# Summing modulation rows over partitions on GpSimd instead of TensorE, in a diffusion trunk layer

## The chip, the cores and the metric

The kernel runs on one core of a Trainium2 chip. The core has TensorE (PE in the profile; PEld is its weight load), VectorE (DVE), ScalarE (ACT), GpSimd (POOL), and SyncE (SP), which here only issues transfers. Each engine works through its own queue in order, and semaphores tie the queues together. The metric is the device time of one execution in microseconds (us), taken as the median of several runs.

## The reference

Two groups of tokens, 128 context tokens and 256 latent tokens, pass through one layer with the same weights. Each group has a conditioning vector, and from it come six modulation rows of 2048 numbers:

```
def modulation(cond, w_mod, b_mod):
    m = jax.nn.silu(cond) @ w_mod + b_mod
    return jnp.split(m[..., None, :], 6, axis=-1)
...
    sh1, sc1, g1, sh2, sc2, g2 = modulation(cond, w_mod_l, b_mod_l)
    h = rms_norm(x, n1) * (1 + sc1) + sh1
    q, k, v, u = project_in(h, w_in_l, qg_l, kg_l)
    attn = attend(q, k, v)
    x = x + g1 * token_mixing(h, attn, u, w_na_proj_l, w_fnet_proj_l, w_gate_l, w_o_l)
    h2 = rms_norm(x, n2) * (1 + sc2) + sh2
    x = x + g2 * swiglu(h2, w_gu_l, w_down_l)
```

Rows 0 and 1 (`sh1`, `sc1`) are needed at once. Rows 2 to 5 (`g1`, `sh2`, `sc2`, `g2`) are needed later, and the change is about these four. A row is a vector times a 2048 x 2048 matrix, for two vectors.

## The kernel before

Nearly all time goes into matmuls of 384 tokens with float32 weights. A product is made in three matmuls (`mm3`, lines 165 to 167): weights and activations are split into a high part (`wh`, `hH`, a rounded copy by ACT, line 161) and a low part (`wl`, `hL`, the rest, subtracted by DVE, line 162), and high times high, high times low and low times high are summed. The weights come in units of 256 x 512 numbers. Before a unit is multiplied, `next_unit` splits the one after it; `wh` and `wl` have three buffers each, so the splitting runs ahead of TensorE by up to two units. A unit is 18 matmuls in most stages.

The stages follow each other: the input projection (with rows 0 and 1 made on TensorE), the gate projection with the Fourier part and the attention woven in, the two branch projections, the output projection with the residual, and the feed-forward part to the end.

The four late rows are made beside these stages. `mod_rows` is a generator: whenever the stage takes a unit, `Paced` advances it by some steps (`RATES`, `CHUNKS`), and each step records a little work in the engines' queues at that place. So the order in each queue is set by where these steps fall. The order of the rows is 2, 4, 3, 5. Each row is made in two parts (`cc`) of 1024 columns, eight parts in all. For a part:

- 16 tiles `wm` of the matrix (128 x 1024, 512 KB each, named `wmr` in the profile) are loaded by SP.
- For each tile and each of the two vectors (`cnd`), DVE multiplies the tile with one number per partition and adds it to the accumulator `acc` (`accr` in the profile, 128 x 2 x 1024), line 347. The first tile only multiplies (line 345).
- TensorE sums the 128 partitions with four matmuls against a tile of ones (line 356); ACT copies the result out of PSUM (line 360), and DVE adds it to `row`, which holds the bias (line 362). `row` was reset by a memset on POOL (line 330) and filled with the bias by four small transfers (line 335).
- POOL issues four transfers of the sums to DRAM, `s_row` (line 367).

Rows 4 and 3 are needed as columns: `columns` loads the row back as 32 x 128 (`colr`, line 373) and TensorE transposes it (line 380) into a PSUM tile, from which DVE writes `msc` or `msh`. Rows 2 and 5 are needed as rows, broadcast to all partitions: `load_rows` has SP load them from `s_row` into `gb` (line 1159), for the output projection and for the end of the feed-forward part. `rows_until` advances the generator until a row is recorded, if a stage needs it before.

Of the kernel before, what the change touches and what calls it, by code (L numbers as in the profile page):

```python
# [6 lines left out]

# [25 lines left out]
CH = 512  # L33
# [15 lines left out]
RATES = [1.5, 0.5, 1.1, 1.07, 0.452]  # L49
# [70 lines left out]
def trunk_kernel(ctx: ExitStack, tc: tile.TileContext, io: dict):  # L120
    nc = tc.nc
# [13 lines left out]
    b_mod = io["b_mod"][0]  # L135
# [20 lines left out]
    def nm(s):  # L156
        return f"{s}{next(ids)}"
# [91 lines left out]
    def new_h(kt):  # L249
# [6 lines left out]
    s_row = {  # L256
        ty: [dram.tile([1, D], F32, tag=f"row{ty}{c}", name=f"s_row{ty}{c}") for c in range(2)] for ty in (2, 3, 4, 5)
    }
# [18 lines left out]
    rows_psum, rows_done = {}, set()  # L277
    rpool = None
# [5 lines left out]
    with ExitStack() as ph:  # L284
# [6 lines left out]
        def at_tile():  # L291
            return pa.tile([P, CH], F32, tag="at", name=nm("at"))
# [8 lines left out]
        def acc_tile():  # L301

            return next(ring)()
# [5 lines left out]
        ROWS = (2, 4, 3, 5)  # L309

        def row_weights():


            def load(ty, cc, k):
                wm = rpool.tile([P, 2, CH], F32, tag="wm", bufs=3, name=nm("wmr"))
                c0 = ty * D + cc * 2 * CH
                nc.sync.dma_start(
                    wm, w_mod[k * P : (k + 1) * P, c0 : c0 + 2 * CH].rearrange("p (i n) -> p i n", i=2)
                )
                return wm  # L320

            return Ahead(load, [(ty, cc, k) for ty in ROWS for cc in range(2) for k in range(KT)], 3)

        def mod_rows(ty, src):


            for cc in range(2):
                acc = rpool.tile([P, 2, 2, CH], F32, tag="acc", name=nm("accr"))
                row = rpool.tile([P, CH], F32, tag="row", name=nm("row"))
                nc.gpsimd.memset(row, 0.0)  # L330
                b = b_mod[ty * D + cc * 2 * CH : ty * D + (cc + 1) * 2 * CH].rearrange("(i n) -> i n", i=2)
                for cnd in range(2):
                    for i in range(2):
                        q = 64 * cnd + 32 * i
                        nc.gpsimd.dma_start(row[q : q + 1], b[i : i + 1])
                for k in range(KT):
                    _, wm = src.take()
                    for cnd in range(2):
                        if cnd:
                            if ty != ROWS[0] or cc + k:  # L340
                                src.more()
                            yield
                        sc = csz[:, k, cnd : cnd + 1]
                        if k == 0:
                            nc.vector.tensor_scalar_mul(acc[:, cnd], wm, sc)
                        else:
                            nc.vector.scalar_tensor_tensor(  # L347
                                out=acc[:, cnd], in0=wm, scalar=sc, in1=acc[:, cnd], op0=ALU.mult, op1=ALU.add
                            )
                    yield  # L350
                yield
                o = rows_psum["tile"]()
                for cnd in range(2):
                    for i in range(2):
                        q = 64 * cnd + 32 * i
                        nc.tensor.matmul(
                            o[q : q + 32], ones, acc[:, cnd, i], start=True, stop=True,
                            tile_position=(0, q), skip_group_check=True,
                        )
                nc.scalar.copy(acc[:, 0, 0], o)  # L360
                yield
                nc.vector.tensor_add(row, row, acc[:, 0, 0])
                for cnd in range(2):
                    for i in range(2):
                        q = 64 * cnd + 32 * i
                        c0 = (2 * cc + i) * CH
                        nc.gpsimd.dma_start(s_row[ty][cnd][:, c0 : c0 + CH], row[q : q + 1])

        def columns(ty):

            r = rpool.tile([32, P], F32, tag="colr", name=nm("colr"))
            for cnd in range(2):
                nc.gpsimd.dma_start(
                    r[16 * cnd : 16 * cnd + 16], s_row[ty][cnd].rearrange("o (k p) -> (o k) p", p=P)
                )
            yield
            yield
            yield
            o = rows_psum["tile"]()
            nc.tensor.transpose(o[:, 0:32], r, ident[:32, :32])  # L380
            ov = o[:, 0:32].rearrange("p (c k) -> p k c", c=2)
            yield
            if ty == 3:
                nc.vector.tensor_copy(msh[1], ov)
                return
            nc.vector.scalar_tensor_tensor(
                out=msc[1], in0=ov, scalar=1.0, in1=ng[:, 1].unsqueeze(2).to_broadcast([P, KT, 2]),
                op0=ALU.add, op1=ALU.mult,
            )
# [5 lines left out]
        def mod_weights(alloc):  # L395


            def load(kt0, n, k0):
                w, nk = n * P, depth_of(n)
                wm = alloc([P, 2, nk, w], "wm")  # L400
                for ty in range(2):
                    col = ty * D + kt0 * P
                    nc.sync.dma_start(
                        wm[:, ty],
                        w_mod[k0 * P : (k0 + nk) * P, col : col + w].rearrange("(k p) n -> p k n", p=P),
                    )
                return wm

            return Ahead(load, [(kt0, n, k0) for kt0, n in MODS for k0 in range(0, KT, depth_of(n))], 0)
# [46 lines left out]
        with ExitStack() as pha:  # L456
# [21 lines left out]
            src = mod_weights(wme)  # L478
# [11 lines left out]
            for j in range(2):  # L490
# [10 lines left out]
                out=csz[:, :, 0:2], in_=pt[:, 0:32].rearrange("p (c k) -> p k c", c=2), func=AF.Silu  # L501
# [5 lines left out]
            for cc in range(4):  # L507
                xT.append(c6([P, 4, TOK], "xT"))
                for k in range(4):
                    o = acc_tile()  # L510
# [3 lines left out]
                for t in (1, 2, 0):  # L514
                    junk = tmp.tile([P, CH], F32, tag="junk", bufs=1, name=nm("junk"))
                    nc.scalar.activation(
                        out=junk, in_=xc[cc][:, t], func=AF.Square, accum_out=ssx[:, t, cc : cc + 1]
# [14 lines left out]
            o = at_tile()  # L532
# [68 lines left out]
            prep = Paced(prepare())  # L601
            rows_psum["tile"] = md_tile

            def rows_and_columns():
                src = row_weights()
                yield
                for ty in ROWS:
                    yield from mod_rows(ty, src)
                    if ty in (3, 4):
                        yield  # L610
                        yield from columns(ty)
                    rows_done.add(ty)
                    yield

            rows = Paced(rows_and_columns(), RATES[0])

            def rows_until(ty):
                while ty not in rows_done:
# [15 lines left out]
            acc = {}  # L634
# [400 lines left out]
        for fc8 in range(8):  # L1035
            po = [mm_tile() for _ in range(NT)]
            sts = []
            for u in range(0, KT, 2):
# [3 lines left out]
                for t in range(NT):  # L1042
                    sl = slice(t * P, (t + 1) * P)
                    for kk in range(2):
                        k = u + kk
# [71 lines left out]
        for f4 in range(4):  # L1117
            gl = [None, None]
            for i, bH, bL in ((1, fH, fL), (0, aH, aL)):
                _, gl[i] = gates.take()  # L1120
                po = [acc_tile() for _ in range(NT)]
                for u in range(0, 8, 2):
# [3 lines left out]
                    for t in range(NT):  # L1126
                        sl = slice(t * P, (t + 1) * P)
                        for kk in range(2):
                            k = u + kk
# [7 lines left out]
        for u in range(0, 10, 2):  # L1137
            wH, wL = next_unit()
            for t in range(NT):
                sl = slice(t * P, (t + 1) * P)  # L1140
                for kk in range(2):
                    k = u + kk
# [73 lines left out]
    for cc in range(4):  # L1216
# [3 lines left out]
        for u in range(0 if cc else 10, KT, 2):  # L1220
# [11 lines left out]
            for t in range(NT):  # L1232
                sl = slice(t * P, (t + 1) * P)
                for kk in range(2):
                    k = u + kk
                    mm3(po[t], mixH[k][:, sl], mixL[k][:, sl], wH[:, kk], wL[:, kk], k == 0, k == KT - 1)
                if u == KT - 2:
# [5 lines left out]
                        out=junk, in_=x2[cc][:, t], func=AF.Square, accum_out=ssx[:, t, cc : cc + 1]  # L1243
# [121 lines left out]
    parts = [([], []) for _ in FF_PARTS]  # L1365
# [143 lines left out]
```

## Time and profile before

| | |
|---|---|
| median of 3 runs | 2027.21 us (2026.4 to 2027.6) |
| profiled execution, its own time | 2027.89 us |
| its span from first to last instruction | 2026.1 us |
| mean granted TensorE clock | 0.997 |
| TensorE (PE) busy | 2004.0 us, 99% |
| VectorE (DVE) busy | 1275.6 us, 63% |
| ScalarE (ACT) busy | 739.0 us, 36% |
| GpSimd (POOL) busy | 43.6 us, 2% |
| transferred | 412.31 MB, mean 203 GB/s |

In rows of groups, a line names the source line, engine, operation, the tiles written and read, shape and count; then follow busy time and the mean of one in ns, and the idle time of the engine just before with what ended it. In rows in order of time, the first two numbers are the start and the duration in us, and what stands in brackets is the idle time ahead and what ended it. A table by stage gives, for each stretch of the span, its length, and each engine's busy time with the number of its instructions, then the granted clock, the mean busy share of the DMA engines and GB/s. Spans on POOL are rough.

### The profile page before, as it was taken

How to read it: one execution, taken by the hardware profiler on the slowest of the kernel's cores; microseconds unless marked ns; L12 is line 12 of the kernel's file. 1: busy time of each engine (PE TensorE's matmuls, PEld its weight loads, DVE VectorE, ACT ScalarE, POOL GpSimd, SP SyncE). 2: the span in 40 equal slices, each digit the busy share in tenths (PEclk: the TensorE clock that was granted, in tenths of full speed). 3: DMA queues.
4: the chain of work that ended last, by engine and by line, in shares of the span. 5: the costliest groups of instructions: out<-in, count | busy, mean ns of one | idle time of the engine just before them, and what ended most of it. 6: DMA issues, size and time to landing. Idle time of an engine off the chain costs nothing.

```text
span 2026.1 us, 24582 instructions
## 1 busy us (share of the span) xinstructions
PE 2004.0 (99%) x9450; PEld 1643.6 (81%) x9450; DVE 1275.6 (63%) x1583; ACT 739.0 (36%) x1078; POOL 43.6 (2%) x92
## 2 busy tenths in 40 slices
PE   7999999999999999999999999999999999999999
PEld 4677888888878888889988888888888888888887
DVE  4646989789998888665855444555555433443653
ACT  4433232445555443334533323322232233232321
POOL 1000000000000000010000000000000000000000
PEclk8999999999999999999999999999999999999999
DMA  9995989677875787854356455556564554455552
GB/s 313 326 343 190 314 271 316 228 230 227 237 205 184 259 284 251 274 188 152 115 167 196 156 172 171 177 159 189 150 197 146 156 150 142 128 163 159 173 182 99
DMA packets 229302, 412.31 MB, mean 203 GB/s; under 512 B 29456, under 2 KB 81696, under 8 KB 229184
## 3 DMA queue, kind: packets, MB, share of 16 engines
q1 hardware_dynamic: 223168, 404.15, 63.2%
q10 hardware_dynamic: 3520, 6.31, 0.9%
q8 instruction: 74, 1.21, 0.2%
q0 software_dynamic: 2496, 0.27, 0.1%
q14 instruction: 44, 0.36, 0.1%
HBM read 382.82 MB, written 31.52 MB: 205 GB/s over the span
## 4 chain that ended last, share of the span: by engine, by line
PE 91%; DMA 4%; DVE 3%; issue 1%; ACT 1%; SPq 0%; DVEq 0%; ACTq 0%
PE mm L165 18%; PE mm L167 18%; PE mm L166 18%; PE at L165 11%; PE at L167 11%; PE at L166 11%; PE at L423 1%; DMA wmr<-in_w_mod 1%; DVE accr L347 1%; DVE wl L162 1%; DMA wraw<-in_w_in 1%; PE at L996 1%; PE at L975 1%; DMA xc<-in_x_prompt 1%; PE at L912 0%
## 5 line engine op out<-in xcount | busy, mean ns | idle before, releaser
L162 DVE TENSOR_TENSOR wl<-wraw,wh 128x1024 fp32r<-128x1024 f32 (+1 forms) x464 | 559.0, 1205 | 643.5 <-ACT wh L161 641.7
L161 ACT CAST wh<-wraw 128x1024 fp32r<-128x1024 f32 (+1 forms) x464 | 481.3, 1038 | 1079.8 <-PE mm L167 660.2
L165 PE MATMUL mm<-wh,hH 128*128 128x512 f32 x1344 | 529.0, 394 | 2.0 <-ACT hH L564 1.2
L167 PE MATMUL mm<-wh,hL 128*128 128x512 f32 x1344 | 524.0, 390 | 0.7 <-DVE hL L162 0.4
L166 PE MATMUL mm<-wl,hH 128*128 128x512 f32 x1344 | 523.6, 390 | 0.8 <-DVE wl L162 0.8
L165 PEld LDWEIGHTS mm<-wh,hH 128*128 128x128 f32 x1344 | 252.3, 188 | 65.9 <-issue 9.1
L347 DVE SCALAR_TENSOR_TENSOR accr<-wmr,csz,accr 128x1024 f32<-128x1024 f32 x240 | 304.3, 1282 | 0.1
L167 PEld LDWEIGHTS mm<-wh,hL 128*128 128x128 f32 x1344 | 252.4, 188 | 55.1 <-DVE hL L162 1.1
L166 PEld LDWEIGHTS mm<-wl,hH 128*128 128x128 f32 x1344 | 252.6, 188 | 51.4 <-DVE wl L162 1.1
L165 PE MATMUL at<-wh,hH 128*128 128x512 f32 x624 | 243.2, 390 | 0.0
L167 PE MATMUL at<-wh,hL 128*128 128x512 f32 x624 | 242.8, 389 | 0.0
L166 PE MATMUL at<-wl,hH 128*128 128x512 f32 x624 | 242.8, 389 | 0.0
L165 PEld LDWEIGHTS at<-wh,hH 128*128 128x128 f32 x624 | 117.1, 188 | 25.8 <-issue 1.7
L167 PEld LDWEIGHTS at<-wh,hL 128*128 128x128 f32 x624 | 117.1, 188 | 24.3
L166 PEld LDWEIGHTS at<-wl,hH 128*128 128x128 f32 x624 | 117.1, 188 | 24.3
L165 PE MATMUL mm<-wh,cH 128*128 128x512 f32 x280 | 109.0, 389 | 0.0
L167 PE MATMUL mm<-wh,cL 128*128 128x512 f32 x280 | 108.9, 389 | 0.0
L166 PE MATMUL mm<-wl,cH 128*128 128x512 f32 x280 | 108.9, 389 | 0.0
L165 PE MATMUL at<-wh,cH 128*128 128x512 f32 x200 | 77.8, 389 | 0.0
L166 PE MATMUL at<-wl,cH 128*128 128x512 f32 x200 | 77.8, 389 | 0.0
L167 PE MATMUL at<-wh,cL 128*128 128x512 f32 x200 | 77.8, 389 | 0.0
L165 PEld LDWEIGHTS mm<-wh,cH 128*128 128x128 f32 x280 | 52.5, 188 | 11.7 <-ACT sg L1385 0.8
(278 smaller groups left out, 1846.0 us busy)
## 6 DMA issues: line engine op xcount, KB each, us to landing
wraw<-in_w_gate_up SPq DMA_DIRECT2D x176, 512.0 KB, 3.7
wmr<-in_w_mod SPq DMA_DIRECT2D x128, 512.0 KB, 5.2
wraw<-in_w_down SPq DMA_DIRECT2D x88, 512.0 KB, 3.7
wraw<-in_w_gate SPq DMA_DIRECT2D x64, 512.0 KB, 4.5
wm<-in_w_mod SPq DMA_DIRECT2D x80, 384.0 KB, 7.0
wraw<-in_w_in SPq DMA_DIRECT2D x56, 512.0 KB, 5.7
wraw<-in_w_o SPq DMA_DIRECT2D x32, 512.0 KB, 5.5
wraw<-in_w_fnet_proj SPq DMA_DIRECT2D x16, 512.0 KB, 6.1
```

The lines of the kernel that those rows point to most:

```text
L161: nc.scalar.copy(H, x)
L162: nc.vector.tensor_sub(L, x, fr(H))
L165: nc.tensor.matmul(out, aH, bH, start=start, stop=False)
L166: nc.tensor.matmul(out, aH, bL, start=False, stop=False)
L167: nc.tensor.matmul(out, aL, bH, start=False, stop=stop)
L347: nc.vector.scalar_tensor_tensor(out=acc[:, cnd], in0=wm, scalar=sc, in1=acc[:, cnd], op0=ALU.mult, op1=ALU.add)
L423: nc.tensor.matmul(pm[q : q + 32, :w], csz[:, k, :], wm[:, ty, kk + par, :], start=k < 2, stop=k >= KT - 2, tile_position=(0, q), skip_gro ...
L975: nc.tensor.transpose(o[:, i * P : (i + 1) * P], sc[:, j, c0 : c0 + P], ident)
L996: nc.tensor.matmul(po[j][:, CTX:TOK].rearrange("p (t q) -> p t q", t=2), w[1 + kc], x.rearrange("p (t b) q -> p t b q", t=2)[:, :, 2 * kc ...
```

## The change

The sum over partitions moves from TensorE to GpSimd: `partition_all_reduce` adds up the 128 partitions of `acc` and writes the sum into all of them, in place, for both vectors at once (128 x 2048). The bias is put in beforehand: `row_sum` resets the whole accumulator on POOL and loads the bias into partition 0, so that the sum contains it. So `row` goes, with the copy by ACT and the addition by DVE, and each multiply on DVE is now a multiply-add. `acc` has two buffers, and the next part's is reset half-way through the present one. The transfers to `s_row` are two of 1024 numbers in place of four of 512. Between the sum and the transposition of rows 4 and 3 stand more steps than before. The scratch memory in which POOL's transfer descriptors are written is set to 8192 bytes per partition, which makes room for the second accumulator.

```
+        def row_sum(ty, cc):
+            acc = rpool.tile([P, 2, 2 * CH], F32, tag="acc", bufs=2, name=nm("accr"))
+            nc.gpsimd.memset(acc, 0.0)
+            b = b_mod[ty * D + cc * 2 * CH : ty * D + (cc + 1) * 2 * CH].rearrange("(o n) -> o n", o=1)
+            for cnd in range(2):
+                nc.gpsimd.dma_start(acc[0:1, cnd], b)
+            return acc
...
                 for k in range(KT):
                     _, wm = src.take()
+                    if k == KT // 2 and n + 1 < len(parts):
+                        ahead = row_sum(*parts[n + 1])
                     for cnd in range(2):
...
-                        if k == 0:
-                            nc.vector.tensor_scalar_mul(acc[:, cnd], wm, sc)
-                        else:
-                            nc.vector.scalar_tensor_tensor(
-                                out=acc[:, cnd], in0=wm, scalar=sc, in1=acc[:, cnd], op0=ALU.mult, op1=ALU.add
-                            )
+                        nc.vector.scalar_tensor_tensor(
+                            out=acc[:, cnd], in0=wm, scalar=csz[:, k, cnd : cnd + 1], in1=acc[:, cnd],
+                            op0=ALU.mult, op1=ALU.add,
+                        )
                     yield
+                nc.gpsimd.partition_all_reduce(acc, acc, P, bass_isa.ReduceOp.add)
+                for cnd in range(2):
+                    nc.gpsimd.dma_start(s_row[ty][cnd][:, cc * 2 * CH : (cc + 1) * 2 * CH], acc[0:1, cnd])
                 yield
-                o = rows_psum["tile"]()
-                for cnd in range(2):
-                    for i in range(2):
-                        q = 64 * cnd + 32 * i
-                        nc.tensor.matmul(
-                            o[q : q + 32], ones, acc[:, cnd, i], start=True, stop=True,
-                            tile_position=(0, q), skip_group_check=True,
-                        )
-                nc.scalar.copy(acc[:, 0, 0], o)
-                yield
-                nc.vector.tensor_add(row, row, acc[:, 0, 0])
...
+                if cc == 1 and ty in (3, 4):
+                    for _ in range(4):
+                        yield
+                    yield from columns(ty)
...
-            yield
-            yield
-            yield
+            for _ in range(4):
+                yield
             o = rows_psum["tile"]()
             nc.tensor.transpose(o[:, 0:32], r, ident[:32, :32])
...
-    nc = bacc.Bacc("TRN2", target_bir_lowering=False, num_devices=1)
+    nc = bacc.Bacc("TRN2", target_bir_lowering=False, num_devices=1, dynamic_dma_scratch_size=8192)
```

TensorE's queue at the end of the first part (row 2, first half; `mm` and `at` are PSUM tiles, `accr` the accumulator), before:

```order
L165 MATMUL mm_2108<-wh_2109,hH_297_1442 128x512
L166 MATMUL mm_2108<-wl_2110,hH_297_1442 128x512
L167 MATMUL mm_2108<-wh_2109,hL_298_1443 128x512
L356 MATMUL at_2199<-accr_1663,ones 32x512 [waits DVE_49]
L356 MATMUL at_2199<-accr_1663,ones 32x512
L356 MATMUL at_2199<-accr_1663,ones 32x512 [waits DVE_49]
L356 MATMUL at_2199<-accr_1663,ones 32x512
L165 MATMUL at_2106<-wh_2134,hH_311_1524 128x512 [waits Activation_49]
L166 MATMUL at_2106<-wl_2135,hH_311_1524 128x512
```

and in the changed kernel, whose lines are numbered one higher there:

```order
L166 MATMUL mm_2106<-wh_2107,hH_297_1442 128x512
L167 MATMUL mm_2106<-wl_2108,hH_297_1442 128x512
L168 MATMUL mm_2106<-wh_2107,hL_298_1443 128x512
L166 MATMUL at_2104<-wh_2134,hH_311_1524 128x512 [waits Activation_49]
L167 MATMUL at_2104<-wl_2135,hH_311_1524 128x512 [waits DVE_49]
```

The four matmuls on the accumulator are gone, here and at the seven other parts; the matmuls around them follow each other as before.

GpSimd's queue at the end of the second part (row 2, second half), before:

```order
L330 MEMSET row_2236 128x512 [waits DMASW6_49,DMASW7_49,DMASW1_49,DMASW0_49]
L335 DMA row_2236<-in_b_mod 1x16x32 [waits Pool_49]
L335 DMA row_2236<-in_b_mod 1x16x32 x3
L367 DMA s_row_99<-row_2236 16x1x32 [waits DMASW2_49,DVE_49]
L367 DMA s_row_99<-row_2236 16x1x32 [waits DMASW3_49]
L367 DMA s_row_100<-row_2236 16x1x32 [waits DMASW4_49]
L367 DMA s_row_100<-row_2236 16x1x32 [waits DMASW5_49]
```

and in the changed kernel, from the load of code ahead of the first sum (the bare ISA row) to the second sum (`accr_1639` and `accr_1918` are the accumulators of the first and second part, `accr_2636` that of the third):

```order
L357 ISA
L357 ISA accr_1639<-accr_1639 128x2048 [waits DMASW3_49,DMASW2_49,DVE_49]
L359 DMA s_row_99<-accr_1639 16x1x64 [waits DMASW6_49,Pool_49]
L359 DMA s_row_100<-accr_1639 16x1x64 [waits DMASW7_49]
L328 MEMSET accr_2636 128x2048 [waits DMASW7_49,DMASW6_49]
L331 DMA accr_2636<-in_b_mod 1x16x64 [waits DMASW0_49,Pool_49]
L331 DMA accr_2636<-in_b_mod 1x16x64 [waits DMASW1_49]
L357 ISA accr_1918<-accr_1918 128x2048 [waits DMASW5_49,DMASW4_49,DVE_49]
```

Each part now has the sum itself (the ISA rows on an accumulator) on GpSimd, which waits for DVE's last multiply-add; the transfers to `s_row` and the reset of the accumulator after next wait behind it.

VectorE's queue at the end of the fourth part (row 4, second half), before; `wl` is the low half of a weight unit, `sc` and `aT` belong to the attention:

```order
L961 TENSOR_SCALAR sc_5126<-sc_5126,sm_5303 128x128 x2
L1005 TENSOR_TENSOR aT_3696<-at_5331,lo_5349 64x384 [waits Activation_49]
L1005 TENSOR_TENSOR aT_3696<-at_5332,lo_5349 64x384 [waits Activation_49]
L347 SCALAR_TENSOR_TENSOR accr_4221<-wmr_5181,csz,accr_4221 128x1024
L162 TENSOR_TENSOR wl_5384<-wraw_5187,wh_5383 128x1024 [waits DMAHW5_49,Activation_49]
L959 RECIPROCAL sm_5371<-sm_5371 128x2
```

and in the changed kernel:

```order
L926 TENSOR_REDUCE mx_5224<-sc_5099 128x2 [waits Activation_49]
L930 TENSOR_REDUCE mx_5224<-sc_5099 128x2 [waits Activation_49]
L352 SCALAR_TENSOR_TENSOR accr_3519<-wmr_5043,csz,accr_3519 128x1024
L163 TENSOR_TENSOR wl_5264<-wraw_5068,wh_5263 128x1024 [waits DMAHW1_49,PE_49,Activation_49]
L926 TENSOR_REDUCE mx_5292<-sc_5099 128x2 [waits DVE_49]
```

The part's last multiply-add, the row on `accr`, moves ahead by two weight units (two `wl` rows), to where the first of the pair at 583.19 us of the trace stood; the transposition of the row keeps its place on TensorE.

More of the change, by code (lines that the diff above doesn't have):

```diff
@@ L8 @@
 import concourse.bass as bass
+import concourse.bass_isa as bass_isa
 import concourse.tile as tile
@@ L322, in row_weights @@
             return Ahead(load, [(ty, cc, k) for ty in ROWS for cc in range(2) for k in range(KT)], 3)
[L324 to L331, printed above, removed]
-                for cnd in range(2):
-                    for i in range(2):
-                        q = 64 * cnd + 32 * i
-                        nc.gpsimd.dma_start(row[q : q + 1], b[i : i + 1])
+        def row_sum(ty, cc):
[5 more added lines that the diff above has]
+            return acc
@@ L336, in mod_rows @@
+        def mod_rows():
+            src = row_weights()
+            parts = [(ty, cc) for ty in ROWS for cc in range(2)]
+            ahead = row_sum(*parts[0])
+            yield
+            yield
+            for n, (ty, cc) in enumerate(parts):
+                acc = ahead
                 for k in range(KT):
                     _, wm = src.take()
+                    if k == KT // 2 and n + 1 < len(parts):
+                        ahead = row_sum(*parts[n + 1])
                     for cnd in range(2):
@@ L339, in mod_rows @@
                         if cnd:
-                            if ty != ROWS[0] or cc + k:
+                            if n + k:
                                 src.more()
                             yield
-                        sc = csz[:, k, cnd : cnd + 1]
-                        if k == 0:
-                            nc.vector.tensor_scalar_mul(acc[:, cnd], wm, sc)
-                        else:
-                            nc.vector.scalar_tensor_tensor(
-                                out=acc[:, cnd], in0=wm, scalar=sc, in1=acc[:, cnd], op0=ALU.mult, op1=ALU.add
-                            )
+                        nc.vector.scalar_tensor_tensor(
+                            out=acc[:, cnd], in0=wm, scalar=csz[:, k, cnd : cnd + 1], in1=acc[:, cnd],
+                            op0=ALU.mult, op1=ALU.add,
+                        )
@@ L350, in mod_rows @@
                     yield
+                nc.gpsimd.partition_all_reduce(acc, acc, P, bass_isa.ReduceOp.add)
+                for cnd in range(2):
+                    nc.gpsimd.dma_start(s_row[ty][cnd][:, cc * 2 * CH : (cc + 1) * 2 * CH], acc[0:1, cnd])
                 yield
-                o = rows_psum["tile"]()
[L353 to L356, printed above, removed]
-                            o[q : q + 32], ones, acc[:, cnd, i], start=True, stop=True,
-                            tile_position=(0, q), skip_group_check=True,
-                        )
@@ L360, in mod_rows @@
-                nc.scalar.copy(acc[:, 0, 0], o)
-                yield
[L362 to L367, printed above, removed]
+                if cc == 1 and ty in (3, 4):
+                    for _ in range(4):
+                        yield
+                    yield from columns(ty)
@@ L369, in columns @@
+                if cc == 1:
+                    rows_done.add(ty)
         def columns(ty):
@@ L375, in columns @@
                 )
-            yield
-            yield
-            yield
+            for _ in range(4):
+                yield
             o = rows_psum["tile"]()
@@ L602, in trunk_kernel @@
             rows_psum["tile"] = md_tile
[L604 to L615, printed above, removed]
+            rows = Paced(mod_rows(), RATES[0])
             def rows_until(ty):
```

## The prediction

> **What bounds the kernel now.** I read the head of the page first, then the busy time by stage, then TensorE's own order of time around the step that the change removes.
>
> ```profile
> span 2026.1 us, 24582 instructions
> PE 2004.0 (99%) x9450; PEld 1643.6 (81%) x9450; DVE 1275.6 (63%) x1583; ACT 739.0 (36%) x1078; POOL 43.6 (2%) x92
> ```
>
> TensorE (PE) is busy 2004.0 of 2026.1 us; VectorE (DVE) has 63%, GpSimd (POOL) 2%. A busy TensorE isn't necessarily one at its pace, and the 63% is a mean over unlike stages, so I take stages and starts:
>
> ```profile
> core 0: us, PE busy (x) PEld busy (x) DVE busy (x) ACT busy (x) POOL busy (x), PEclk, DMA share, GB/s
> 165.00:250.00 85.00, 85.00 (x376) 70.23 (x375) 73.50 (x78) 27.48 (x33) 2.37 (x5) 1.00 0.78 261
> 250.00:350.00 100.00, 100.00 (x445) 81.86 (x445) 91.44 (x104) 31.50 (x35) 4.65 (x9) 1.00 0.87 290
> 350.00:460.00 110.00, 108.37 (x549) 91.35 (x548) 87.19 (x117) 51.76 (x91) 4.46 (x9) 1.00 0.76 238
> 460.00:600.00 140.00, 139.37 (x755) 114.10 (x754) 131.59 (x194) 77.10 (x172) 4.47 (x9) 1.00 0.78 228
> 730.00:900.00 170.00, 169.19 (x762) 137.75 (x761) 129.16 (x151) 62.64 (x87) 4.46 (x9) 1.00 0.76 252
> 1300.00:1600.00 300.00, 300.00 (x1328) 247.48 (x1327) 156.81 (x156) 85.00 (x91) 4.46 (x9) 1.00 0.54 165
> ```
>
> From 165 us on TensorE loses under 2 us in any of these stages, at full clock (1.00). DVE is second, and close: 131.59 of 140 us (94%) in the attention stage, 91% from 250 to 350, about half after 1300. So a microsecond taken off TensorE counts, and one added to DVE counts only where DVE's lead over TensorE is used up. POOL waits nearly always.
>
> **The change, part by part.** *Eight sums leave TensorE.* The first and the seventh in TensorE's order of time (start, duration):
>
> ```profile
> 252.10 0.39 PE L166 MATMUL mm<-wl,hH 128*128 128x512 f32 x1
> 252.33 0.39 PE L167 MATMUL mm<-wh,hL 128*128 128x512 f32 x1
> 252.65 1.07 PE L356 MATMUL at<-accr,ones 128*32 128x512 f32 x8
> 253.64 0.50 PE L165 MATMUL at<-wh,hH 128*128 128x512 f32 x1
> 253.98 0.39 PE L166 MATMUL at<-wl,hH 128*128 128x512 f32 x1
> ...
> 1300.42 0.39 PE L167 MATMUL mm<-wh,hL 128*128 128x512 f32 x1
> 1300.74 1.06 PE L356 MATMUL at<-accr,ones 128*32 128x512 f32 x8
> 1301.73 0.50 PE L165 MATMUL mm<-wh,cH 128*128 128x512 f32 x1
> 1302.07 0.39 PE L166 MATMUL mm<-wl,cH 128*128 128x512 f32 x1
> ```
>
> Matmuls start 0.23 us apart (252.10, 252.33). From L167 to the second matmul behind the sum two steps, 0.46, would do; it takes 253.98 - 252.33 = 1.65, and 1302.07 - 1300.42 = 1.65 likewise. A sum costs 1.65 - 0.46 = 1.19 us of TensorE, and eight cost **9.5 us**. No other matmul goes, and only one transpose of `colr` is reordered.
>
> *DVE and ACT.* The rows of the accumulator (min/median/max in ns):
>
> ```profile
> L347 DVE SCALAR_TENSOR_TENSOR accr<-wmr,csz,accr x240: 1275/1280/1298, 187.8 to 1589.9; 128x1024 f32<-128x1024 f32 x120
> L345 DVE TENSOR_SCALAR accr<-wmr,csz x16: 747/750/754, 183.6 to 1320.6; 128x1024 f32<-128x1024 f32 x16
> L360 ACT COPY accr<-at x8: 586/587/591, 253.8 to 1609.1; 128x512 f32<-128x512 f32 x8
> L362 DVE TENSOR_TENSOR row<-row,accr x8: 681/684/687, 260.3 to 1619.7; 128x512 f32<-128x512 f32 x8
> L356 PE MATMUL at<-accr,ones x64: 592/605/617, 252.6 to 1608.4; 128*32 128x512 f32 x64
> ```
>
> The first multiply of a part becomes a multiply-add: 16 x (1.28 - 0.75) = +8.5 us of DVE. The bias add goes: 8 x 0.68 = -5.5. DVE gets 3 us more in all, 0.38 per part; ACT loses 8 x 0.59 = 4.7. I cost both at nothing: weights are split ahead (next fence), and 0.38 us fits into that lead. With the lead used up, 3 us would come back.
>
> *What GpSimd gets.* No row shows a sum over partitions on POOL. The nearest:
>
> ```profile
> L330 POOL MEMSET row<- 128x512 f32 x8 | 4.3, 532 | 176.1 <-PE at L439 156.0 <-DMA s_row<-row 20.0
> ```
>
> 532 ns for 512 elements per partition is 2.1 us for one sweep over 2048. Below: one sweep, 2.1. Above: a read, a write and seven halvings of 128 partitions, nine sweeps, 19 us. I take the middle, D = 10.5 us, since nothing lies near either end; it is an estimate. The memset is now 2.1 us too, so POOL gains about 8 x (10.5 + 1.6) = 97 us on an engine that idles; its DMAs halve (16 bias and 16 row transfers in place of 32 and 32). The two buffers give a reset a whole part's time; the first accumulator alone is reset and given its bias just before use:
>
> ```profile
> 164.89 0.53 POOL L330 MEMSET row<- 128x512 f32 x1 [156.01 <-PE at L439]
> ...
> DMA to landing us min/median/max: 1.5/3.3/7.4
> ```
>
> 164.9 + 2.1 + two issues of 0.5 + at most 7.4 to land is 175.4; DVE's first multiply is at 183.6 (above), so it costs nothing. The same holds for the code that POOL must load once for the new instruction (the bare ISA row in its order): it stands ahead of the first sum, where POOL idles 93.64 us (a row below). The halved scratch for POOL's descriptors meets two issues at a time where four stood. Row 5 is wanted last:
>
> ```profile
> L1159 SPq DMA_DIRECT2D gb<-s_row x16: 320/418/527, 826.6 to 1877.3; - x16
> ```
>
> SP issues that load some 250 us after the last sum (1608.4, above), so nothing queued on SP waits for it.
>
> *The new wait.* TensorE waits in its queue for the transposed row, and everything behind it waits too. For row 4:
>
> ```profile
> 583.19 2.48 DVE L347 SCALAR_TENSOR_TENSOR accr<-wmr,csz,accr 128x1024 f32<-128x1024 f32 x2
> ...
> 605.25 1.91 POOL L367 DMA_DIRECT2D s_row<-row  x4 [113.11 <-DVE row L362]
> 607.82 0.48 POOL L373 DMA_DIRECT2D colr<-s_row  x1 [0.65 <-DMA s_row<-row]
> 608.76 0.48 POOL L373 DMA_DIRECT2D colr<-s_row  x1 [0.46 <-issue]
> 615.23 0.25 PE L380 MATMUL at<-ident,colr 32*128 32x32 f32 x1
> ```
>
> In the new order row 4's last multiply-add stands where the first of the pair at 583.19 stood, so it ends near 584.4; the transpose keeps its place at 615.2. Of the 30.8 us between, the row's way to its transposable form took 615.23 - 605.25 = 10.0 at most. So D may reach 20.8 us before TensorE waits; above that row 4 costs D - 20.8. At D up to 19 it is nothing.
>
> *Does the sum disturb DVE?* This decides the sign. DVE prepares `wl` ahead; near the last part:
>
> ```profile
> 1588.76 1.23 DVE L162 TENSOR_TENSOR wl<-wraw,wh 128x1024 fp32r<-128x1024 f32 x1 [2.86 <-ACT wh L161]
> 1589.90 1.28 DVE L347 SCALAR_TENSOR_TENSOR accr<-wmr,csz,accr 128x1024 f32<-128x1024 f32 x1
> ...
> 1591.75 1.05 ACT L161 CAST wh<-wraw 128x1024 fp32r<-128x1024 f32 x1 [3.02 <-PE at L167]
> ...
> 1595.86 0.39 PE L166 MATMUL mm<-wl,hH 128*128 128x512 f32 x1
> ...
> 1599.94 0.39 PE L166 MATMUL mm<-wl,hH 128*128 128x512 f32 x1
> ```
>
> The `wl` that ends at 1589.99 is used at 1595.86. The next follows the cast that ends at 1592.8, is used one unit (4.08 us) later, at 1599.94, and needs 1.23: it may start as late as 1598.7. A hold from the end of the multiply-add, 1591.2, is covered for 1598.7 - 1591.2 = **7.5 us**; each microsecond beyond stalls TensorE. I use 7.5 for all eight parts. The one sign of sharing between the engines in this trace:
>
> ```profile
> 261.05 1.42 DVE L345 TENSOR_SCALAR accr<-wmr,csz 128x1024 f32<-128x1024 f32 x2
> 261.31 2.21 POOL L367 DMA_DIRECT2D s_row<-row  x4 [93.64 <-DVE row L362]
> 268.13 1.91 POOL L335 DMA_DIRECT2D row<-in_b_mod  x4 [0.29 <-POOL row L330]
> ```
>
> Four DMA issues of POOL took 2.21 us beside DVE's fast multiply, and 1.91 where none ran: there POOL loses 0.3. DVE lost nothing to POOL's memsets and issues (the 240 multiply-adds lie between 1275 and 1298 ns). But none of those reads a tile, and the sum does. The price lies between nothing and a full hold, 8 x (D - 7.5).
>
> The Trainium skill speaks against the change here: "SBUF — State Buffer", section "Who interferes with whom", says that a DVE instruction with two SBUF inputs contends with a GpSimd instruction that reads SBUF, and that whoever comes first has the shared ports for the whole instruction. By it the sum would be the first rival's; the row at 261.31 agrees only that a port is shared, and no run here shows a reading GpSimd instruction.
>
> I take nothing: DVE's multiply-adds and subtractions show no loss to POOL, and most of a sum over partitions is passing values between partitions rather than reading the tile.
>
> **Sum.** The profiled execution took 2027.9 us, 1.8 beyond its span. 2027.9 - 9.5 = 2018.4; the median of the runs, 2027.2, lies 0.7 lower, so **2017.7 us**.
>
> **Rivals.** *DVE is held out (slower).* Place: the first `wl` behind each part's last multiply-add. With D = 10.5 eight holds cost 8 x 3.0 = 24.0, net +14.5: 2041.7. At D = 19: 8 x 11.5 = 92, net +82.5: 2109.7. It decides from D = 7.5 + 1.19 = 8.7 us; below that the gain outweighs it. For it: DVE at 91 to 94% where four parts end leaves little to catch up with. Against: no row of it.
>
> *Nothing comes of it.* DVE turns bound where it is fullest, and the extra 0.38 per part with the displaced order take back the four parts up to 600 us: 4 x 1.19 + 3 = 7.8 of the 9.5, so 2025.5. Against: the 0.00 to 1.63 us that TensorE lost in those stages.
>
> *The transpose waits.* D = 30: row 4 costs 9.2, and the later row 3, placed alike, hardly more than that again; 2027 to 2036.
>
> *The sum is far longer.* At D = 200 eight sums take 1600 us behind each other, from 250 on; row 5 would be ready 1850 + its transfers, and row 4, fourth in the queue, at 1050 instead of 605: some 435 us of TensorE waiting, about 2450. The trace has nothing for it. The Trainium skill, "GPSIMD Engine Reference", section 3.2, gives 247.7 us for a reduction along partitions at 128 x 2048; by that price this rival would hold, with row 4 at 250 + 4 x 247.7 = 1241 (an estimate). It is another instruction, and no run here shows either.
>
> **How the numbers follow.** DVE undisturbed, or held for less than its cover: 0.50, own range 2015.5 (2 us better, for the freed ACT copies and PSUM tiles) to 2022. Held out beyond the cover: 0.38. Nothing: 0.07. Transpose waits: 0.03. Far longer: 0.02. The range 2015.5 to 2070 takes in the hold up to D = 14 (8 x 6.5 - 9.5 = +42.5); it leaves out longer holds (about 0.12), the last rival and a little below. What differs by less than 0.2%, 4 us, a measurement of this kernel can't tell from no change. Faster 0.51, same 0.07, slower 0.42.
>
> **What would show it.** Right: no matmul on `accr`, TensorE's count 64 lower, L165 to L167 0.23 us apart past each part's end, `wl` starting on time beside the sum. Wrong: TensorE idle behind `wl` some 8 us after each part's last multiply-add, with a gap on DVE as long as POOL's sum; or idle at the transpose of `colr`. A sum over 8.7 us decides nothing unless DVE stands still beside it.

## The result, and the profile after

The changed kernel takes **2051.38 us** (median of 4 runs, 2050.59 to 2058.54) against 2026.81 for the kernel before: 1.0129 times as long, 95% interval 1.0117 to 1.0141. The forecast was 2017.7 us and faster. It went to the other side of no change, 9.7 us above the price of the first rival, "DVE is held out". The forecast range reached up to 2070 us to take in that rival, and so contains the time.

The head of the page after:

```profile
span 2048.8 us, 24378 instructions
PE 1999.5 (98%) x9386; PEld 1644.5 (80%) x9386; DVE 1335.2 (65%) x1575; ACT 734.9 (36%) x1070; POOL 135.2 (7%) x68
```

TensorE issues 64 matmuls fewer and is 4.5 us less busy, so the sums did leave it; but the span is 22.7 us longer. DVE is busy 59.6 us more with 8 instructions fewer, and only 3 of the 59.6 us were foreseen: its instructions have become longer. What TensorE waits for (the view of the waits: us in total, times, longest), before:

```profile
PE at L499 <- DMA rows_c<-in_c: 5.3, 1, 5.3
PE at L975 <- DVE sc L961: 2.2, 2, 1.6
...
PE mm L166 <- DVE wl L162: 0.8, 1, 0.8
```

and after, where the same lines are numbered otherwise:

```profile
PE at L497 <- POOL ident masks.py:199: 10.4, 1, 10.4
PE mm L167 <- DVE wl L163: 9.8, 5, 4.0
PE at L962 <- DVE sc L948: 9.7, 5, 3.9
...
PE at L167 <- DVE wl L163: 1.4, 1, 1.4
PE at L168 <- DVE uL L163: 1.4, 1, 1.4
```

Two waits have appeared. TensorE waits for DVE, for `wl` and `sc` above all: 22.3 us in these four rows, where it was 3.0. And the first matmul waits 10.4 us for GpSimd's identity matrix, where it waited 5.3 for a transfer.

The cause of the first is seen beside a sum. GpSimd, DVE and TensorE at the end of the seventh part, in order of time:

```profile
1305.45 12.13 POOL L357 PARTITION_ALL_REDUCE accr<-accr  x1 [378.67 <-DVE accr L352]
```

```profile
1302.93 1.23 DVE L163 TENSOR_TENSOR wl<-wraw,wh 128x1024 fp32r<-128x1024 f32 x1 [2.85 <-ACT wh L162]
1304.08 1.28 DVE L352 SCALAR_TENSOR_TENSOR accr<-wmr,csz,accr 128x1024 f32<-128x1024 f32 x1
...
1307.01 8.89 DVE L163 TENSOR_TENSOR wl<-wraw,wh 128x1024 fp32r<-128x1024 f32 x1 [1.17 <-ACT wh L162]
...
1316.30 1.21 DVE L163 TENSOR_TENSOR wl<-wraw,wh 128x1024 fp32r<-128x1024 f32 x1
```

```profile
1313.89 0.39 PE L166 MATMUL mm<-wh,hH 128*128 128x512 f32 x1
1315.96 0.50 PE L167 MATMUL mm<-wl,hH 128*128 128x512 f32 x1 [1.69 <-DVE wl L163]
```

The same subtraction takes 1.23 us ahead of the sum, 8.89 while it runs and 1.21 behind it. It is recorded as busy, not as waiting, so a look at DVE's idle time doesn't find it: it has to be looked for in durations. It ends at 1315.90, and the matmul that needs it starts at 1315.96, 2.07 us after the one ahead of it in place of 0.23.

Every part has one such instruction. In the rows of two groups (minimum, median and maximum of a duration in ns):

```profile
L352 DVE SCALAR_TENSOR_TENSOR accr<-wmr,csz,accr x256: 1271/1280/7395, 186.8 to 1603.9; 128x1024 f32<-128x1024 f32 x128
L357 POOL PARTITION_ALL_REDUCE accr<-accr x8: 11872/11876/12772, 255.9 to 1605.3; - x8
```

The median multiply-add is what it was; one of 256 takes 7.4 us. With six `wl` (7.9 to 9.3 us) and one small TENSOR_SCALAR of 128 x 24 (7.6 us, median 0.18) these are eight held instructions, 58.2 us beyond their usual durations, nearly all of DVE's 59.6.

### The profile page after: what moved, and what is told of

It reads as the page before. It is cut to its first block, busy times and chain, and to the rows that moved or that the text cites. A ratio compares the mean times of both kernels' runs of the same rounds, so it can differ in the third digit from the quotient of the medians.

```text
span 2048.8 us, 24378 instructions
## 1 busy us (share of the span) xinstructions
PE 1999.5 (98%) x9386; PEld 1644.5 (80%) x9386; DVE 1335.2 (65%) x1575; ACT 734.9 (36%) x1070; POOL 135.2 (7%) x68
## 4 chain that ended last, share of the span: by engine, by line
PE 83%; DVE 9%; issue 3%; DMA 3%; ACT 1%; POOL 0%; SPq 0%; ACTq 0%; DVEq 0%; POOLq 0%
PE mm L166 17%; PE mm L167 17%; PE mm L168 17%; PE at L167 10%; PE at L168 10%; PE at L166 10%; DVE wl L163 3%; DVE accr L352 3%; PE at L421 1%; DMA wm<-in_w_mod 1%; ACT wh L162 1%; DMA wraw<-in_w_in 1%; DMA wmr<-in_w_mod 0%; PE at L962 0%; DMA gb<-s_row 0%
## 5 line engine op out<-in xcount | busy, mean ns | idle before, releaser
L163 DVE TENSOR_TENSOR wl<-wraw,wh 128x1024 fp32r<-128x1024 f32 (+1 forms) x464 | 603.1, 1301 | 606.4 <-ACT wh L162 605.2
L352 DVE SCALAR_TENSOR_TENSOR accr<-wmr,csz,accr 128x1024 f32<-128x1024 f32 x256 | 330.4, 1304 | 0.1
L166 PEld LDWEIGHTS mm<-wh,hH 128*128 128x128 f32 x1344 | 253.6, 189 | 64.8 <-issue 7.0
L167 PEld LDWEIGHTS mm<-wl,hH 128*128 128x128 f32 x1344 | 253.7, 189 | 60.6 <-DVE wl L163 10.1
L357 POOL PARTITION_ALL_REDUCE accr<-accr x8 | 96.2, 12020 | 1295.5 <-DVE accr L352 1295.5
```

What stands on the lines that cost most here:

```text
L163: nc.vector.tensor_sub(L, x, fr(H))
L166: nc.tensor.matmul(out, aH, bH, start=start, stop=False)
L167: nc.tensor.matmul(out, aH, bL, start=False, stop=False)
L352: nc.vector.scalar_tensor_tensor(out=acc[:, cnd], in0=wm, scalar=csz[:, k, cnd : cnd + 1], in1=acc[:, cnd], op0=ALU.mult, op1=ALU.add,)
L357: nc.gpsimd.partition_all_reduce(acc, acc, P, bass_isa.ReduceOp.add)
```

## The experiments

The theory to test, **H**: the sum reads SBUF, the memory in which the tiles lie, and while it does, DVE's instructions that need two inputs from SBUF stand still; TensorE pays what DVE's lead doesn't cover. The rivals: the changed order or the extra work of DVE costs the time; or any long work of GpSimd does. A lag in what follows is the start of the same matmul in a kernel less that in the kernel before, both counted in TensorE's order with the sums and transposes left out.

**The sum left out.**

```
-                nc.gpsimd.partition_all_reduce(acc, acc, P, bass_isa.ReduceOp.add)
```

> The sum over partitions is left out; everything else of the change stays, so the rows that are written hold only partition 0's share. Theory H (DVE is held while GpSimd's sum reads the tile, about 29 us in all, and about 3 us come from a late start of the identity behind a code load): both go and the 9.5 us of TensorE stay saved: 2017.7 us, 2015.5 to 2020. Rival O (the changed order of the steps and DVE's 3 us more are what costs): still above 2040. Rival P (GpSimd's longer queue delays what waits for it, sum or not): between 2025 and 2040.

2017.25 us, ratio 0.9951 (0.9936 to 0.9965). In its trace TensorE's lag falls by 1.2 us at each of the eight places. So the saving on TensorE is as large as it was worked out, and the 34 us between this kernel and the changed one come with the sum, those of the start among them.

**The sum back on TensorE, in the changed frame** (double accumulator, bias ahead, new order).

```
-                nc.gpsimd.partition_all_reduce(acc, acc, P, bass_isa.ReduceOp.add)
+                nc.tensor.matmul(o[q : q + 32], ones, a4[:, cnd, i], ...)   # four, as before
```

> The changed kernel with its bias put in beforehand, its two accumulators, its steps and its smaller scratch, but the sum is made on TensorE by the four matmuls on the ones as before, and copied by ACT. Theory H: all of the loss hangs on GpSimd's sum, so this is the kernel before within what can be measured: 2027 us, 2024 to 2030. Rival O (order of the steps, DVE's extra multiply-adds): 2040 to 2055.

2028.91 us, ratio 1.0012 (1.0003 to 1.0021): order, resets and longer first multiplies cost some 2 us together. That rival falls.

**Memsets in place of the sum**, seven of 128 x 2048, so that GpSimd works as long but only writes.

```
-                nc.gpsimd.partition_all_reduce(acc, acc, P, bass_isa.ReduceOp.add)
+                for _ in range(7):
+                    nc.gpsimd.memset(acc, 0.0)
```

> In place of the sum stand seven memsets of the accumulator on GpSimd, 7 x 1.81 = 12.7 us per part, longer than the sum's 11.9, and they only write; the rows are zero. Theory H (it is the reading that holds DVE): like without the sum, 2017.7 us, 2015.5 to 2021. Rival B (any instruction of GpSimd that runs so long holds DVE): 2045 to 2060. Rival P (what waits for GpSimd's queue): the same as with the sum, near 2050.

2023.68 us, ratio 0.9984 (0.9974 to 0.9994): 6 us above H's number and outside what it gave. The tiles' rows show both halves:

```profile
L352 DVE SCALAR_TENSOR_TENSOR accr<-wmr,csz,accr x256: 1273/1279/1287, 182.9 to 1579.1; 128x1024 f32<-128x1024 f32 x128
...
L949 DVE TENSOR_SCALAR sc<-sc,sm x48: 280/419/2041, 446.5 to 654.1; 128x384 f32<-128x384 f32 x32, 128x128 f32<-128x128 f32 x16
```

No multiply-add is held by a writing GpSimd, and no `wl`. But the TENSOR_SCALAR that scales `sc` in the attention, from SBUF to SBUF, is: eight of 48 take 1.6 to 2.0 us in place of 0.28 or 0.42, and each ends within 0.3 us of the end of a memset. TensorE's lag grows by 4.9 us at these two places, which is most of the 6 us above H's number. So writing alone doesn't hold instructions with two inputs, as H says, and a second kind of conflict exists beside it; it may be what holds the 128 x 24 instruction above. No other instruction of GpSimd that reads was run: that it is the reading, and not something else in the sum, is inferred.

**The sum made twice**, one behind the other.

```
+                nc.gpsimd.partition_all_reduce(acc, acc, P, bass_isa.ReduceOp.add)
```

> The sum is made twice on the same tile, one after the other, so the rows are 128 times too large. Theory H: a second hold of about 9 us per part, none of it covered any more: 8 x 9 = 72 us on top of 2051, 2123 us, 2100 to 2145. Rival O: no more than the changed kernel, 2050 to 2056, but for a wait of the two transposes of up to 12 us each. Rival P: 2051 to 2075.

2116.14 us, ratio 1.0438 (1.0422 to 1.0454). The second sums add 64.8 us, a mean of 8.1, of 11.9 that they run. By the lag it is 6.5 to 11.9 us at seven parts, where DVE's lead is used up already, and 0.1 at the last. Multiply-adds take as much as 10.1 us:

```profile
L352 DVE SCALAR_TENSOR_TENSOR accr<-wmr,csz,accr x256: 1269/1278/10146, 188.2 to 1669.8; 128x1024 f32<-128x1024 f32 x128
```

**The start.** GpSimd's first rows, before and after:

```profile
1.01 0.29 POOL masks.py:199 TENSOR_SCALAR_AFFINE_SELECT ident<-ident 128x128 f32<-128x128 f32 x1
```

```profile
10.02 0.28 POOL masks.py:199 TENSOR_SCALAR_AFFINE_SELECT ident<-ident 128x128 f32<-128x128 f32 x1 [9.08 <-issue]
```

The instruction that makes the identity matrix waits 9.08 us on nothing that the profile shows. Two kernels ask why. The first takes the instruction away:

```
-    make_identity(nc, ident)
+    nc.sync.dma_start(ident, io["identity"])
```

> The changed kernel with one edit: the identity matrix is loaded from a table in memory by a DMA of SyncE, so GpSimd's AFFINE_SELECT that made it is gone, and with it the 9.1 us for which that instruction stood idle at the start (first matmul at 10.36 us, 5.26 in the kernel before). Theory H (the sums hold VectorE, and the start costs a code load): the first matmul is back near 5.3 us, TensorE's start is 3 to 5 us earlier, the holds stay: 2048.2 us (2046 to 2049.5). Rival S (the late start is hidden, since transfers of weights set the pace of the first stage): 2051, and TensorE's lag against the kernel before at 165 us is the same 3 us as in the changed kernel.

The second leaves it, but has GpSimd make a tiny sum before it:

```
+    nc.gpsimd.memset(tiny, 0.0)
+    nc.gpsimd.partition_all_reduce(tiny, tiny, P, bass_isa.ReduceOp.add)   # 128 x 1
     make_identity(nc, ident)
```

> The changed kernel with a sum of 128x1 zeros put ahead of the identity; nothing else changes. Theory C (code that GpSimd has loaded stays loaded over the end of an execution, and AFFINE_SELECT is in the sum's code too, so that a program that asks for the sum's code alone finds it loaded): the first GpSimd instruction isn't late, AFFINE_SELECT starts before 5 us plus the tiny sum, first matmul at 5.3 to 8 us, 2048 us (2046 to 2050). Rival L (each execution loads the code anew): AFFINE_SELECT still starts at 9 to 12 us, and 2051 (2050 to 2053).

They took 2049.58 us (ratio 1.0108, 1.0092 to 1.0125) and 2045.15 us (1.0094, 1.0079 to 1.0109). In the second, GpSimd starts at once:

```profile
0.98 0.38 POOL L240 PARTITION_ALL_REDUCE tiny<-tiny  x1
1.23 0.27 POOL masks.py:197 MEMSET ident<- 128x128 f32 x1
1.58 0.29 POOL masks.py:199 TENSOR_SCALAR_AFFINE_SELECT ident<-ident 128x128 f32<-128x128 f32 x1
```

The sum starts at 0.98 us without a wait, though its code is asked for only 0.1 us ahead of it (by MODIFY_POOL_CONFIG at 0.85 and 0.89 us, of GpSimd's sequencer; in the changed kernel the same pair stands at 0.96 and 0.99 us, ahead of the wait of 9.08). That is theory C: the code is still loaded from the execution ahead, and a kernel pays at its start if it ends with another set of code than it begins with. L would have it wait. At 200 us the two kernels lag by -1.0 and -2.5 us, the changed kernel by +3.2. But the first gains only 1.8 us in its median (the second 6.2): from there to the end its lag grows by 23.2 us (to 22.2), that of the changed kernel by 19.5 (to 22.7). What a hold costs seems to depend on where it falls among DVE's work.

**A tiny sum alone**, in the kernel before, recorded where the modulation rows begin, at some 165 us. It waits for nothing there, so GpSimd comes to it earlier: its code is asked for at 17.86 us, and it runs at 24.38 us, after a wait of 6.70 us.

```
+                nc.gpsimd.partition_all_reduce(tiny, tiny, P, bass_isa.ReduceOp.add)   # 128 x 1
```

> The kernel before with a single sum of 128x1 zeros put at the point where the modulation rows begin (some 165 us), which leaves all work on TensorE. Theory H (the start's delay comes from the program's using two sets of GpSimd code, and VectorE's holds from the size of the sums): AFFINE_SELECT at the start waits some 9 us as in the changed kernel, first matmul near 10.4 us, and the time is 3.2 us longer: 2030 us (2028 to 2032); the tiny sum holds nothing that shows. Rival S (a late start is hidden): 2026.5, within 1.5 us of the kernel before.

2045.95 us, ratio 1.0089 (1.0072 to 1.0106). The start is late as H says (AFFINE_SELECT waits 8.83 us), the lag at 590 us is 2.9; but at the end it is 15.0, with no wait to account for it. The reason is TensorE's own pace, for stretches of about 100 us. By stage (length, TensorE's busy time and number of matmuls, and the same for the other engines, then the granted clock, the DMA share and GB/s), the kernel before and this one:

```profile
1100.00:1150.00 50.00, 50.00 (x222) 41.39 (x222) 21.88 (x18) 17.76 (x22) 0.00 (x0) 1.00 0.50 159
```

```profile
1050.00:1100.00 50.00, 50.00 (x223) 41.39 (x221) 26.23 (x26) 14.24 (x16) 0.00 (x0) 1.00 0.63 188
1100.00:1150.00 50.00, 50.00 (x217) 40.51 (x216) 22.78 (x21) 18.04 (x22) 0.00 (x0) 1.00 0.48 156
```

217 matmuls in 50 us in place of 222, at a granted clock of 1.00. Two more kernels: the same once more, and the tiny sum put ahead of the identity, as above, in the kernel before.

> The kernel before with a sum of 128x1 zeros at some 165 us, a second time, since its first runs lost 12 us in stretches of about 100 us in which matmuls started 0.234 us apart. Theory T (these stretches were a state of that chip at that time): no such stretches, the late start alone, 2030 us (2028 to 2032). Rival P (they belong to the program): 2043 us (2041 to 2049).

> The kernel before with a sum of 128x1 zeros ahead of the identity, and nothing else. Theory C (GpSimd's code stays loaded, and a program that asks for one set of code alone pays nothing): first matmul at 5.3 to 6 us, 2026.6 us (2025 to 2028). Rival P (the 12 us that the kernel with a tiny sum at 165 us lost in stretches where matmuls started 0.234 us apart in place of 0.227 come from having a sum in this program): such stretches here too, 2038 us (2034 to 2042).

The first took 2044.26 us, ratio 1.0084 (1.0069 to 1.0099), so the loss is the program's and not the hour's (its profile is of a far longer execution, so the stretches themselves weren't seen a second time). The second took 2024.15 us, ratio 0.9987 (0.9978 to 0.9996), with an early start (a lag of -3.8 us at 200 us) and no such stretches; C holds there too. Nor has the changed kernel any, whose start is late as well. Why the one program has them is open.

**All sums in quarters**, each behind a marker that DVE writes two units of work later, so that a hold fits into DVE's lead; the identity from a table.

```
+                if i:
+                    nc.vector.memset(token, 1.0)
+                    nc.gpsimd.memset(token, 0.0)
+                nc.gpsimd.partition_all_reduce(piece, piece, P, bass_isa.ReduceOp.add)
+                if i < 4 - 1:
+                    for _ in range(2):
+                        yield
```

> The changed kernel with the sum of a part in four pieces of 512 columns, spaced over VectorE's following work (each piece behind the first waits for a marker that VectorE writes two units of work later), and the identity loaded as a table. Theory H (a hold costs only what it exceeds VectorE's lead by, 7.5 us at the last part): a piece of a quarter's size takes some 3.5 us and holds for less, each is covered, so the holds cost nothing or a few us: 2019 us (2016 to 2024), which is faster than both kernels. Rival F (a sum has a large fixed price, so a piece takes over 7 us as well): 8 x 4 holds, 2050 to 2150. Rival R (it is the held time in all that costs, whatever the lead): 2046 to 2050.

2035.38 us, ratio 1.0040 (1.0025 to 1.0055), between H's number and the rivals'. A quarter does hold for about a quarter (2.0 us at most, where a whole sum held for 6.1 to 8.1). The lag is -0.4 at 400 us, +11.3 at 640, and from there it falls with each part, to +5.1. The rise lies in the attention, where DVE was busy 94% of the time before, but the holds are only a part of it. 5.9 us of it are one step, at 637 us, where TensorE waits 4.78 us for a tile that DVE splits (`pt`): the last piece of the fourth part has ended 20 us earlier, and DVE, busy without a pause, has multiply-adds of the next part in its queue ahead of that tile. This kernel finishes its parts earlier (the last multiply-add starts at 1424.8 us, not 1603.9), so that from 600 to 640 us it makes nine multiply-adds, where the changed kernel makes one: some 10 us more of DVE's work. What share is due to that wasn't separated.

**Only the last four parts on GpSimd**, the first four as in the kernel before, with the tiny sum first: whole, and in quarters one unit apart.

```
+                late = ty in ROWS[2:]
...
+                if late:
+                    nc.gpsimd.partition_all_reduce(...)     # whole, or four pieces with a marker between
```

> The first four parts (rows 2 and 4, which end while VectorE is 87 to 94% busy) are summed on TensorE as in the kernel before, the last four (rows 3 and 5, VectorE at 52 to 76%) on GpSimd as in the changed kernel; a sum of 128x1 zeros ahead of the identity, so that the start isn't late. Theory F (a hold costs what VectorE can't make good out of idle time; in the changed kernel TensorE fell 19.1 us back over the first four parts and 0.4 over the last four): 2026.6 + 0.4, less about 1 for the start, 2026 us (2024 to 2028). Rival E (each sum costs the same, a quarter of 19.5 / 2): 2026.6 + 9.8 - 1 = 2035.4 us (2033 to 2038).

2030.52 us, ratio 1.0019 (1.0010 to 1.0028): between the theories, above F's bounds and below E's. The lag rises by 0.7, 4.7, 0.7 and 0.7 us at the four sums, net of what each saves. Three of them are a hold that is a little longer than the lead; the second shows a second loss behind the first, DVE and then TensorE at 895 to 912 us:

```profile
895.39 8.63 DVE L163 TENSOR_TENSOR wl<-wraw,wh 128x1024 fp32r<-128x1024 f32 x1 [1.66 <-ACT wh L162]
```

```profile
904.08 0.50 PE L167 MATMUL mm<-wl,hH 128*128 128x512 f32 x1 [1.43 <-DVE wl L163]
...
909.81 0.50 PE L166 MATMUL mm<-wh,hH 128*128 128x512 f32 x1 [1.58 <-ACT wh L162]
911.07 0.80 PE L167 MATMUL mm<-wl,hH 128*128 128x512 f32 x1 [0.76 <-DVE wl L163]
```

The held `wl` delays what stands behind it on DVE (the residual, `d` and `x`), so the next units are split late as well.

> As the kernel with the last four parts on GpSimd, and each of these four sums made in four pieces of 512 columns, one unit of work apart (a piece behind the first waits for a marker that VectorE writes after that unit). Theory F: a piece holds VectorE some 2 us, less than its lead there, so the saving of 4 x 1.19 us stays: 2026.6 - 4.8, less about 1 for the start, 2020.8 us (2018.5 to 2023), faster than both kernels. Rival R (the held time in all costs, as long in pieces as in one): as the kernel with whole sums, 2026.

**2019.01 us** (2018.39 to 2019.83), ratio 0.9961 (0.9949 to 0.9974): faster than both kernels. GpSimd and DVE at the first quarter of the seventh part, and the tile's row:

```profile
1277.00 3.47 POOL L380 PARTITION_ALL_REDUCE accr<-accr  x1 [350.92 <-DVE accr L368]
```

```profile
1278.56 2.00 DVE L163 TENSOR_TENSOR wl<-wraw,wh 128x1024 fp32r<-128x1024 f32 x1 [1.19 <-ACT wh L162]
```

```profile
L380 POOL PARTITION_ALL_REDUCE accr<-accr x16: 3232/3234/3471, 729.5 to 1663.5; - x16
```

`wl` loses 0.8 us in place of 7.7. The lag falls by 1.2 us at three of the four parts, and by 0.1 at the second, where a quarter holds the residual's addition for some 1.6 us: 3.7 of the 7.8 us gained. The rest of the gain is no work of the sums: 1.5 us are a wait for `wl` at 840 us that is gone, and the profiled execution was 4.1 us ahead at 200 us already. The fairer comparison is with the kernel before that has the same tiny sum in front: 2024.15 us, so 5.1 us are gained, the 3.7 and the 1.5.

This doesn't tell the hold's length from the held time in all, since pieces hold less in all too: 4.2 us in place of 29.8. The changed kernel itself does: its first four holds and its last four are 29.1 us each, and they cost TensorE 23.9 and 5.2 us (worked out below). It is the hold's length against DVE's lead at the place that decides.

## Why the prediction was wrong, step by step

**The saving on TensorE: right.** 9.5 us were forecast; past each part's end two steps of 0.23 us stand where 1.65 us stood. The kernel without the sum came out at 2017.25, the forecast at 2017.7.

**D, the length of a sum: near.** 10.5 us estimated, 11.88 measured (median), and inside the bounds of 2.1 and 19.

**"I take nothing" for DVE beside the sum: the step that failed.** This term of the sum stood at 0 and measured 29.0 us (worked out below). The rows that the prediction leaned on (multiply-adds between 1275 and 1298 ns beside memsets and issues) were of GpSimd work that doesn't read a tile. The prediction said so and then took the value that they showed. The reason given, that a sum mostly passes values rather than reads its tile, had no row behind it, and the held rows speak against it. Such an instruction stands still while the sum runs, except for the last 2.9 us of the sum's recorded time: the `wl` above ends at 1315.90, needs 1.2, and so was let go near 1314.7, 9.2 us after the sum's start at 1305.45. The Trainium skill, "SBUF — State Buffer", section "Who interferes with whom", had the rule that the prediction cited and then set aside, and the trace agrees with it. Here 8 of 8 sums hold an instruction that reads twice from SBUF or a TENSOR_SCALAR between SBUF tiles, while four multiply-adds with one input in PSUM and a reduction with one input from SBUF, the first two rows here, run inside the third sum (480.09 to 492.86 us) at their usual durations, until the multiply-add on the accumulator is held:

```profile
481.03 1.66 DVE L911 SCALAR_TENSOR_TENSOR sc<-at,rq,bp 128x256 f32<-128x256 f32 x4
482.60 0.95 DVE L926 TENSOR_REDUCE mx<-sc 128x2 f32<-128x768 f32 x1
...
483.79 7.39 DVE L352 SCALAR_TENSOR_TENSOR accr<-wmr,csz,accr 128x1024 f32<-128x1024 f32 x1
```

**The lead of 7.5 us, used for all eight parts: right where it was read, wrong elsewhere.** There 9.2 - 7.5 = 1.7 us; in three of the last four parts TensorE's step of 0.23 behind `wl` becomes 1.8 to 2.1. The rival's formula, so corrected, gives 8 x 1.7 = 13.6. But the changed kernel's lag grows by 19.1 us over the first four parts (3.2 to 22.3) and by 0.4 over the last four (to 22.7). With 4 x 1.19 saved in each half, the holds cost 23.9 and 5.2 us, **29.0 in all**. The prediction named DVE's 91 to 94% where four parts end (its own table has 79% for one of these stages), and still took the lead from the last part, where DVE is at about half. As it stood, with the length of the whole sum, the rival's formula gives 8 x (11.88 - 7.5) = 35.0 and 2052.7 us, near the measured 2051.4. That is luck: a hold is 2.7 us shorter than the sum, the first four cost 6.0 us each and the last four 1.3, and the late start isn't in the formula.

**The code load: half right.** The load ahead of the first sum is hidden, as said. What was missed, and so stood at nothing in the sum, is that asking for the sum's code makes the identity's code be loaded at the next start: the lag of 3.2 us in the profile. How much of the median that is isn't exact: at 200 us three profiled executions with a late start lag by 3.2 to 4.6 us, and nine with an early start by -0.7 to -4.1.

**The rest: right.** No row came late (`colr` is transposed without a wait), and DVE's longer first multiplies and the order cost some 2 us.

**The sum again:** 2027.9 - 9.5 + 29.0 + 3.2 = 2050.6, the time of the profiled execution. It is reached because the 29.0 is worked out from the same lags; what tests it are the kernels above. Of the first-named forecasts for these twelve kernels, four times fell inside their bounds: without the sum, with it on TensorE, with it twice, and with the last four in quarters. The other eight missed theirs by 0.1 to 14 us. The largest misses are the two kernels with the tiny sum behind the start, for a reason that is open, and the one with all sums in quarters, where DVE's work was brought forward.

## What to carry to other kernels

Before work goes to an idle engine, ask what it reads and writes: here an engine with 2% of its time used stopped one at 94%. To a first estimate such a hold costs its length less the lead of the held engine at that place, so read the lead in every stage where it falls and not in the quietest; cut the work into pieces shorter than the lead, and put them where the held engine has idle time (here the last four sums in quarters, 2019.0 us). Where a duration of some neighbour is the evidence, check that it does to the port in question what the new instruction will do.

## What was not expected of the hardware

- GpSimd's loaded code outlives an execution: with two sets of code in a program the first instruction that needs the other set waits 8.8 to 9.4 us in all four profiled executions of that kind; with one set alone, even the sum starts at 0.98 us.
- A hold goes both ways: in the kernel with all sums in quarters, pieces take 3.2 us, or 4.1 where a multiply-add or `wl` is already running when they start (3232, 3486 and 4194 ns, minimum, median and maximum).
- A sum over 128 partitions costs by its columns: 3.23 us for 512, 11.88 for 2048, hence by estimate 0.35 us and 5.6 ns for each column; the tiny one of a single column took 0.38.
- In a program with one tiny sum behind the start, TensorE was slower, without a wait, by 2% in stretches of 100 us. Beside its usual times it had single executions of 11546 and 7169 us. The profile of the latter shows every matmul long:

```profile
L166 PE MATMUL mm<-wh,hH 128*128 128x512 f32 x1344 | 1480.8, 1102 | 1.2 <-ACT hH L565 1.2
```

The mean matmul takes 1.1 us there, where it is 0.39. Nothing that was run tells why.
